# Modulation pieces used a step behind their load in a one-core decoder layer

## The chip, the core and the metric

One core of a Trainium2 chip runs the whole layer as one program. The metric is the device time of one execution in microseconds.

## What is computed

One layer of a hybrid decoder, batch 1, 256 tokens, width 2048, all in float32:

```python
mod = (jax.nn.silu(c) @ w_ada + b_ada)[:, None, :]
sh1, sc1, g1, sh2, sc2, g2 = jnp.split(mod, N_MOD, axis=-1)
h = rms_norm(x, norm1_g) * (1.0 + sc1) + sh1
proj = h @ w_in
...
mixed = jnp.concatenate([rms_norm(attn, attn_out_g), rms_norm(ssm, ssm_out_g)], axis=-1) @ w_out
x = x + g1 * mixed
h2 = rms_norm(x, norm2_g) * (1.0 + sc2) + sh2
ff = jnp.square(jax.nn.relu(h2 @ w_ff1)) @ w_ff2
return x + g2 * ff
```

Between `proj` and `mixed` stand a windowed attention of 8 heads and a state-space branch with a scan. `w_ada` is 2048 x 12288, `w_in` 2048 x 4096, `w_out` 2048 x 2048, `w_ff1` 2048 x 8192 and `w_ff2` 8192 x 2048. The weights come from HBM once, 296 MB in all, 100 MB of them `w_ada`, whose product has a single row.

## The kernel before

**The weights' way.** A load of weights is 512 KB, 128 partitions of 1024 float32. SP issues its DMA into a ring of five buffers with the tag `raw` (`raw`, L176). ACT copies it rounded into `wh` (`copy`, L161), DVE writes the remainder into `wl` (`sub`, called by `split`, L172; the row stands at L136), and PE multiplies with both. So a buffer of the ring is held from the issue of its DMA until DVE has taken `wl` from it. `w_in` is worked off in parts of two loads and 24 matmuls (`w_in_part`, L330), `w_out`, `w_ff1` and `w_ff2` in chunks of one load, 24 matmuls in `pair_bank` (L864) or 16 in `pair_part` (L856). There are 256 feed-forward chunks.

**The modulation.** `w_ada` comes in 96 pieces of 1 MB, four to a block of 512 columns; in this document [b,g] is piece g of block b. They are not loaded in one go but spread over the whole program: `pump` (L285) takes the next pieces of `ADA_ORDER`, and `pump_at(i)` (L578) does so at the rate `PUMPS[i]` for each step of stage i. A piece is loaded into two `raw` buffers, or into one large buffer that is free in that stage (`RINGS`: `PD`, `HA`, `U`, `WB`, or the two halves in `T0`), and used at once: for the blocks in `PE_BLOCKS` by four matmuls of 512 columns (L254), for the others by a scalar_tensor_tensor on DVE with a running sum (L274, whose rows stand at L158).

**The order.** Each engine works its instructions in a fixed order that a scheduler has set when the program was built; an instruction that waits holds up all behind it on its engine. `tc.issue_after(x)` ties an instruction behind x on the same engine.

**The stages.** First the norm of x and the first blocks of `mod` (to 47 us in the profile), then `w_in` against `h`, which `make_h` (L317) makes from x in four groups of 512 channels. From 224 us the scan of the state-space branch runs on DVE beside the last `w_in` parts. Then `y_block` (L693) multiplies the states on PE (L697 and L701), and the attention follows (`att_scores`, L708; `att_values`, L740). `branch_scale` (L831) norms and splits each branch into `CA`, `Q` and `K` for `w_out`. The second norm needs all of `w_out`. Then `ff1_half` (L942) makes the first half of 16 `w_ff1` pairs in eight PSUM banks each, `ff1` the rest, and the four groups of `ff2` follow. `mod` of the last block is needed at the start of the fourth group.

Of the kernel before, what the change touches and what calls it, by code (L numbers as in the profile page):

```python
# [1 line left out]

# [14 lines left out]
P = 128  # L17
SEQ = 256
# [98 lines left out]
class _K:  # L117
    def __init__(self, nc, tc, I, out, pools):
        self.nc, self.tc, self.I, self.out = nc, tc, I, out
        self.sb, self.ps = pools  # L120
        self.n = 0

    def t(self, tag, shape, dt=F32, bufs=1):
        self.n += 1
        return self.sb.tile(list(shape), dt, name=f"{tag}_{self.n}", tag=tag, bufs=bufs)

# [64 lines left out]
    def mm3(self, ps, xh, xl, wh, wl, start, stop):  # L191
        mm = self.nc.tensor.matmul
        mm(ps, xh, wh, start=start, stop=False)  # L193
        mm(ps, xh, wl, start=False, stop=False)  # L194
        mm(ps, xl, wh, start=False, stop=stop)  # L195


def _body(nc, tc, I, out, sb, ps):
# [47 lines left out]
    def ada_pieces(b):  # L246
        c4 = slice(4 * b, 4 * b + 4)
        if b in PE_BLOCKS:
            acc = tr()
            for g in range(4):  # L250
                q = 0
                for raw in ada_raw(I["w_ada"][b, g]):
# [6 lines left out]
                if g < 3:  # L259
                    yield  # L260
            rows = t("rows", [P, NB], bufs=2)
            copy(rows, acc)
            pc = tr()
            for j in range(4):
                mm(pc[:, j : j + 1], rows[:, 128 * j : 128 * j + 128], ones, start=True, stop=True)
            add(mod[:, c4], pc[:, 0:4], col["b_ada"][:, c4])
        else:
            part = t("adap", [P, 2, 4], bufs=2)
            for j in range(4):
                o = 0  # L270
                for i, raw in enumerate(ada_raw(I["w_ada"][b, j])):
                    n = raw.shape[1] * NB
                    rf = raw.rearrange("p a n -> p (a n)")
                    stt(rf, rf, 1.0, cbc[:, o : o + n], ALU.mult, ALU.mult, accum=part[:, i, j : j + 1])  # L274
                    o += n
                if i:
                    add(part[:, 0, j : j + 1], part[:, 0, j : j + 1], part[:, 1, j : j + 1])
                if j < 3:
                    yield
            add(mod[:, c4], part[:, 0], col["b_ada"][:, c4])  # L280
        yield

    state = {"left": 96, "gen": None, "due": 0.0}

    def pump(n=1, until=None):  # L285
        while n > 0 and state["left"] > (96 - until if until is not None else 0):
            if state["left"] % 4 == 0:
                state["gen"] = ada_pieces(ADA_ORDER[24 - state["left"] // 4])
            next(state["gen"])
            state["left"] -= 1  # L290
            n -= 1

    pump(3)

    rw = t("HB", [P, 4, SEQ])
    onek, sel = rw[:, 3, 0:32], rw[:, 3, P : 2 * P]
# [18 lines left out]
    hs = {}  # L315

    def make_h(kg):  # L317
        hs[kg] = t("HA" if kg % 2 == 0 else "HB", [P, 2, 4, SEQ], F32R)
# [522 lines left out]

    xss = branch_scale(("CA",), yg, col["sog"], sq2, 2)
    pump(99, until=48)
    z = t("XT", [P, 16, SEQ])
    for j in range(4):
        nc.sync.dma_start(z[:, 4 * j : 4 * j + 4], I["xT"][:, 4 * j : 4 * j + 4])
# [9 lines left out]
    def pair_part(pp, src, xs, first, last):  # L856
        hi, lo = load_p(src)
        for e in range(2):
            for kk in range(4):
                mm(pp[e], hi[:, e, kk], xs[kk].rearrange("p s n -> p (s n)"), start=first and kk == 0, stop=False)  # L860
            for kk in range(4):
                mm(pp[e][:, 0:SEQ], lo[:, e, kk], xs[kk][:, 0], start=False, stop=last and kk == 3)  # L862

    def pair_bank(bank, src, xs, first, last):  # L864
        hi, lo = load_p(src)
        for e in range(2):
            o = bank[:, SEQ * e : SEQ * e + SEQ]
            for kk in range(4):
                mm(o, hi[:, e, kk], xs[kk][:, 0], start=first and e + kk == 0, stop=False)  # L869
                mm(o, hi[:, e, kk], xs[kk][:, 1], start=False, stop=False)  # L870
            for kk in range(4):
                mm(o, lo[:, e, kk], xs[kk][:, 0], start=False, stop=last and e + kk == 4)  # L872


    def w_out_pair(half, x8, np_):
# [41 lines left out]

    def make_h2(kg):
        pump(99, until=56 + 8 * kg)
        c4 = slice(4 * kg, 4 * kg + 4)  # L920
# [21 lines left out]
    def ff1_half(base):  # L942
# [7 lines left out]
        for i in range(8):  # L950
            copy(part[base + i], banks[i])

    def ff1(np_):
        pp = [k.acc(), k.acc()]
        if np_ % 2 == 0:
            pump(1)
# [3 lines left out]
        aa = ff1_slot(np_)  # L960
# [7 lines left out]
        stt(v, v, 0.0, v, ALU.max, ALU.mult)  # L968
        copy(aa[:, :, 0], v)
        sub(aa[:, :, 1], v, aa[:, :, 0].bitcast(F32))  # L970

    def ff2(G, np_):
        pp = [k.acc(), k.acc()]
# [16 lines left out]

    ff1_half(0)
    ff1_half(8)
    make_h2(2)
    make_h2(3)
    for np_ in range(8):
        ff1(np_)
    y2 = [t("WB2", [P, 8, SEQ]), t("WB3", [P, 8, SEQ])]
    y2 = [y2[c // 8][:, c % 8] for c in range(16)]
    for G in range(4):
# [2 lines left out]
                ff1(8 * G + 8 + np_)  # L1002
        if G == 3:
            pump(99)
            for c in range(16):
                stt(y2[c], y2[c], mod[:, 80 + c : 81 + c], z[:, c], ALU.mult, ALU.add)
        for np_ in range(8):
# [25 lines left out]
```

## Time and profile before

| | us |
|---|---|
| median of three runs | 1293.12 |
| lowest and highest | 1277.10, 1297.98 |
| the profiled execution | 1291.11 |
| its span in the trace | 1289.3 |

The mean granted clock of TensorE over the span is 0.948 of full speed. In the profile's rows a name is that of a tile with its number left out, so `raw<-w_ada` is any load of a piece of `w_ada` into the ring. What stands in square brackets behind a timeline's row is the engine's idle time before it and what released it. In a windows row the order is PE, PEld (weight loads), DVE, ACT, POOL, then the granted clock, the share of the DMA engines and GB/s.

### The profile page before, as it was taken

How to read it: one execution, taken by the hardware profiler on the slowest of the kernel's cores; microseconds unless marked ns; L12 is line 12 of the kernel's file. 1: busy time of each engine (PE TensorE's matmuls, PEld its weight loads, DVE VectorE, ACT ScalarE, POOL GpSimd, SP SyncE). 2: the span in 40 equal slices, each digit the busy share in tenths (PEclk: the TensorE clock that was granted, in tenths of full speed). 3: DMA queues.
4: the chain of work that ended last, by engine and by line, in shares of the span. 5: the costliest groups of instructions: out<-in, count | busy, mean ns of one | idle time of the engine just before them, and what ended most of it. 6: DMA issues, size and time to landing. Idle time of an engine off the chain costs nothing.

```text
span 1289.3 us, 18892 instructions
## 1 busy us (share of the span) xinstructions
PE 1193.7 (93%) x7330; PEld 1012.5 (79%) x7330; DVE 910.5 (71%) x1499; ACT 579.0 (45%) x792; POOL 13.0 (1%) x12
## 2 busy tenths in 40 slices
PE   4688899998998799789989999999999999999998
PEld 1456677863777699789978888888888888888887
DVE  5977697899534985668799655975576666667564
ACT  3588644332145544334354444453344443344432
POOL 1100000000000000000000000000000000000000
PEclk9798999997679899989999999999999999999999
DMA  9785898779155665658997666766677666767663
GB/s 371 286 317 186 280 333 287 274 267 385 36 179 180 239 193 175 210 182 297 327 326 252 203 191 216 262 212 182 195 236 240 225 187 190 219 222 227 202 212 95
DMA packets 77705, 299.64 MB, mean 232 GB/s; under 512 B 8624, under 2 KB 10928, under 8 KB 71856
## 3 DMA queue, kind: packets, MB, share of 16 engines
q1 hardware_dynamic: 77616, 298.45, 69.1%
q8 instruction: 57, 0.93, 0.3%
q14 instruction: 32, 0.26, 0.0%
HBM read 296.31 MB, written 2.10 MB: 231 GB/s over the span
## 4 chain that ended last, share of the span: by engine, by line
PE 60%; DMA 15%; DVE 15%; ACT 5%; issue 4%; SPq 0%; ACTq 0%; DVEq 0%
PE acc L860 31%; PE acc L862 15%; DMA raw<-w_ada 10%; DVE wl L136 4%; DVE raw L158 3%; DVE T L136 2%; PE acc L872 2%; PE acc L870 2%; PE acc L869 2%; PE acc L701 1%; DMA raw<-w_ff 1%; ACT wh L161 1%; PE acc L697 1%; DVE XT L136 1%; ACT TO L161 1%
## 5 line engine op out<-in xcount | busy, mean ns | idle before, releaser
L161 ACT ACTIVATE wh<-raw 128x1024 fp32r<-128x1024 f32 x360 | 381.3, 1060 | 502.1 <-PE acc L860 290.8
L136 DVE TENSOR_TENSOR wl<-raw,wh 128x1024 fp32r<-128x1024 f32 x360 | 439.7, 1223 | 219.0 <-ACT wh L161 217.2
L158 DVE SCALAR_TENSOR_TENSOR raw<-raw,cbc 128x1024 f32<-128x1024 f32 x98 | 119.6, 1225 | 49.3 <-DMA raw<-w_ada 49.0
L860 PE MATMUL acc<-CA,wh 128*128 128x512 f32 x512 | 139.7, 398 | 6.4 <-DVE rows L136 3.4
L860 PEld LDWEIGHTS acc<-CA,wh 128*128 128x128 f32 x512 | 88.4, 190 | 19.2 <-ACT wh L161 4.5
L862 PEld LDWEIGHTS acc<-CA,wl 128*128 128x128 f32 x512 | 76.7, 189 | 10.7
L862 PE MATMUL acc<-CA,wl 128*128 128x256 f32 x512 | 78.2, 278 | 0.0
L860 PE MATMUL acc<-WB,wh 128*128 128x512 f32 x256 | 70.2, 396 | 0.0
L860 PE MATMUL acc<-TO,wh 128*128 128x512 f32 x256 | 70.0, 394 | 0.0
L193 PE MATMUL acc<-wh,HA 128*128 128x512 f32 x128 | 49.8, 417 | 13.2 <-ACT HA L161 9.2
L194 PE MATMUL acc<-wl,HB 128*128 128x512 f32 x128 | 52.6, 411 | 7.1 <-DVE wl L136 7.0
L194 PE MATMUL acc<-wl,HA 128*128 128x512 f32 x128 | 53.2, 416 | 0.9 <-DVE wl L136 0.9
L195 PE MATMUL acc<-wh,HB 128*128 128x512 f32 x128 | 50.6, 400 | 0.0
L195 PE MATMUL acc<-wh,HA 128*128 128x512 f32 x128 | 50.5, 406 | 0.0
L193 PE MATMUL acc<-wh,HB 128*128 128x512 f32 x128 | 47.5, 403 | 1.7 <-ACT wh L161 1.7
L860 PEld LDWEIGHTS acc<-WB,wh 128*128 128x128 f32 x256 | 43.5, 188 | 5.6
L860 PEld LDWEIGHTS acc<-TO,wh 128*128 128x128 f32 x256 | 43.4, 188 | 5.5
L862 PEld LDWEIGHTS acc<-WB,wl 128*128 128x128 f32 x256 | 39.1, 188 | 5.9
L862 PEld LDWEIGHTS acc<-TO,wl 128*128 128x128 f32 x256 | 38.9, 188 | 5.8
L193 PEld LDWEIGHTS acc<-wh,HA 128*128 128x128 f32 x128 | 25.1, 198 | 22.4 <-ACT HA L161 9.3
L862 PE MATMUL acc<-WB,wl 128*128 128x256 f32 x256 | 40.8, 281 | 0.0
L862 PE MATMUL acc<-TO,wl 128*128 128x256 f32 x256 | 39.8, 277 | 0.0
(322 smaller groups left out, 2352.0 us busy)
## 6 DMA issues: line engine op xcount, KB each, us to landing
raw<-w_ff SPq DMA_DIRECT2D x256, 512.0 KB, 4.3
raw<-w_ada SPq DMA_DIRECT2D x98, 512.0 KB, 5.2
raw<-w_in SPq DMA_DIRECT2D x64, 512.0 KB, 6.0
raw<-w_out SPq DMA_DIRECT2D x32, 512.0 KB, 3.8
HA<-w_ada SPq DMA_DIRECT2D x11, 1024.0 KB, 7.3
PD<-w_ada SPq DMA_DIRECT2D x9, 1024.0 KB, 4.9
Q<-w_ada SPq DMA_DIRECT2D x5, 1024.0 KB, 10.3
K<-w_ada SPq DMA_DIRECT2D x5, 1024.0 KB, 8.7
```

What stands on the lines that cost most here:

```text
L136: return (eng or self.nc.vector).tensor_tensor(out, a, b, op=op)
L158: self.nc.vector.scalar_tensor_tensor(out, a, s, b, op0=op0, op1=op1, accum_out=accum)
L161: self.last_act = self.nc.scalar.activation(out, a, AF.Copy, scale=scale).ins
L193: mm(ps, xh, wh, start=start, stop=False)
L194: mm(ps, xh, wl, start=False, stop=False)
L195: mm(ps, xl, wh, start=False, stop=stop)
L697: mm(pv[:, r - r8], toep[:, r].rearrange("p g s j -> p (g s j)"), u2[:, :, r, :], start=True, stop=False)
L860: mm(pp[e], hi[:, e, kk], xs[kk].rearrange("p s n -> p (s n)"), start=first and kk == 0, stop=False)
L862: mm(pp[e][:, 0:SEQ], lo[:, e, kk], xs[kk][:, 0], start=False, stop=last and kk == 3)
L869: mm(o, hi[:, e, kk], xs[kk][:, 0], start=first and e + kk == 0, stop=False)
L870: mm(o, hi[:, e, kk], xs[kk][:, 1], start=False, stop=False)
L872: mm(o, lo[:, e, kk], xs[kk][:, 0], start=False, stop=last and e + kk == 4)
```

## The change

A piece of `w_ada` is now made in two steps. `ada_piece` issues the load and stops; its use follows at the next call of `pump`, or when `drain` is called: ahead of every tile whose tag is in `PLACES`, in `make_h` and `make_h2`, and behind each `pump` with an `until`. The use is tied behind the last main matmul (PE) or the last split's subtraction (DVE) that has been written by then. The tag `T0` is no longer a place for pieces, and the last rate is 0.4 instead of 0.5.

```diff
-RINGS = (('Q', 'K'), ('raw',), ('T0', 'PD', 'raw', 'raw'), ('T0', 'raw', 'raw'), ('raw',), ('HA', 'U', 'WB0'), ('HA', 'PD'))
-PUMPS = (2.0, 2.0, 1.0, 1.0, 1.0, 1.0, 1.0, 0.5, 0.5, 2.5, 1.0, 2.0, 1.0, 0.5)
+PLACES = ("Q", "K", "U", "V", "TO", "CA", "PD", "HA", "WB0")
+RINGS = (('Q', 'K'), ('raw',), ('PD', 'raw', 'raw'), ('raw',), ('raw',), ('HA', 'U', 'WB0'), ('HA', 'PD'))
+PUMPS = (2.0, 2.0, 1.0, 1.0, 1.0, 1.0, 1.0, 0.5, 0.5, 2.5, 1.0, 2.0, 1.0, 0.4)
...
     def split(self, hi, lo, v):
         self.copy(hi, v)
-        return self.sub(lo, v, hi.bitcast(F32))
+        r = self.sub(lo, v, hi.bitcast(F32))
+        self.last_split = r.ins
+        return r
...
+    def ada_piece(b, g):
         c4 = slice(4 * b, 4 * b + 4)
+        raws = ada_raw(I["w_ada"][b, g])
+        yield
         if b in PE_BLOCKS:
...
+            with behind("last_main"):
+                for raw in raws:
...
         else:
...
+            with behind("last_split"):
+                for i, raw in enumerate(raws):
...
     def pump(n=1, until=None):
+        drain()
         while n > 0 and state["left"] > (96 - until if until is not None else 0):
-            if state["left"] % 4 == 0:
-                state["gen"] = ada_pieces(ADA_ORDER[24 - state["left"] // 4])
-            next(state["gen"])
+            drain()
+            i = 96 - state["left"]
+            piece = ada_piece(ADA_ORDER[i // 4], i % 4)
+            next(piece)
+            pending.append(piece)
```

`make_h` takes three steps to a channel group of 128 where it took four:

```diff
             v = xTf[:, kc]
-            mul(v, v, rbc)
-            nc.scalar.activation(v, v, AF.Identity, bias=mod[:, kc : kc + 1], scale=g1c[:, kc : kc + 1])
-            end = k.split(hs[kg][:, 0, kc % 4], hs[kg][:, 1, kc % 4], v)
+            sh = mod[:, kc : kc + 1]
+            stt(v, v, g1c[:, kc : kc + 1], rbc, ALU.mult, ALU.mult)
+            hi = hs[kg][:, 0, kc % 4]
+            k.last_act = nc.scalar.activation(hi, v, AF.Identity, bias=sh).ins
+            end = nc.vector.scalar_tensor_tensor(
+                hs[kg][:, 1, kc % 4], v, sh, hi.bitcast(F32), op0=ALU.add, op1=ALU.subtract
+            )
```

The second half of the first eight `w_ff1` pairs is done in eight PSUM banks, a quarter of the depth for all eight and then the next, with `pump_at(13, 80)` in each step:

```diff
+    def ff1_rest(base):
+        banks = [tr() for _ in range(4)] + [k.acc() for _ in range(4)]
+        for kg in range(2, 4):
+            make_h2(kg)
+            for i in range(8):
+                pair_bank(banks[i], I["w_ff1"][base + i, kg], h2[4 * kg : 4 * kg + 4], kg == 2, kg == 3)
+                pump_at(13, 80)
+        for i in range(8):
+            v = t("rows", [P, 2, SEQ], bufs=2)
+            add(v.rearrange("p e n -> p (e n)"), banks[i], part[base + i])
+            ff1_square(v, base + i)
...
-    make_h2(2)
-    make_h2(3)
-    for np_ in range(8):
-        ff1(np_)
+    ff1_rest(0)
```

**Three places in the order of the engines.** The first is PE at the `y_block`s. Before, in front of them and into the first (`cpad` marks a piece, here [12,0] to [12,2]; the first L701 row is the first block's; `Q`, `K` and the L725 and L726 rows are `att_scores(0)`):

```order
L254 MATMUL tr_2624<-WB_453_2625,cpad_77 32x512 x4
L713 MATMUL tr_2674<-ident_70,Q_818 128x128 x4
L713 MATMUL tr_2680<-ident_70,K_1230 128x128 x4
L254 MATMUL tr_2624<-HA_2764,cpad_77 32x512 x4
L725 MATMUL tr_2687<-WB_430_2423 128x128
L726 MATMUL tr_2687<-WB_430_2423 128x256
L725 MATMUL tr_2699<-WB_430_2423 128x128
L726 MATMUL tr_2699<-WB_430_2423 128x256
L254 MATMUL tr_2624<-U_2830,cpad_77 32x512 x4
L701 MATMUL acc_2439<-XT_1776,CA_378 64x64 x4
L697 MATMUL acc_2439<-PD_1773,TO_374 128x64
L701 MATMUL acc_2439<-XT_1776,CA_378 64x64 x4
```

Now, from the end of the first block to the middle of the second:

```order
L729 MATMUL acc_2414<-PD_1753,TO_370 128x64
L733 MATMUL acc_2414<-XT_1756,CA_374 64x64 x4
L271 MATMUL tr_2456<-HA_2412,cpad_77 32x512 x4
L271 MATMUL tr_2456<-U_2461,cpad_77 32x512 x4
L271 MATMUL tr_2456<-WB_438_2467,cpad_77 32x512 x4
L733 MATMUL acc_2475<-XT_1756,CA_374 64x64 x4
L729 MATMUL acc_2475<-PD_1753,TO_370 128x64
L733 MATMUL acc_2475<-XT_1756,CA_374 64x64 x4
L729 MATMUL acc_2475<-PD_1753,TO_370 128x64
L733 MATMUL acc_2475<-XT_1756,CA_374 64x64 x4
```

Before, the four pieces of block 10 stood among the last `w_in` matmuls and those of block 11, then [12,0] to [12,2], between these and the first L701; now [10,0] to [10,2] stand behind the first block, [10,3] to [11,3] further on among the blocks, and `att_scores(0)` and [12,0] to [12,2] behind the last one.

The second is DVE at the first `branch_scale`, where `PD` and `HA` with `adap` are pieces of block 13 and `rs` is the norm of the branch. Before:

```order
L158 SCALAR_TENSOR_TENSOR PD_3622,adap_3621<-PD_3622,cbc_72 128x2048
L136 TENSOR_TENSOR T_455_2673<-T_455_2673 128x512
L152 TENSOR_SCALAR rs_2427<-tr_3169 128x2
L166 RECIPROCAL rs_2427<-rs_2427 128x2
L136 TENSOR_TENSOR rs_2427<-rs_2427 128x2 x2
L152 TENSOR_SCALAR rs_2427<-rs_2427 128x2
L136 TENSOR_TENSOR rs_2427<-rs_2427 128x2
L829 COPY rbc_3193<-tr_3194 128x256
L156 SCALAR_TENSOR_TENSOR WB_463_2713<-WB_463_2713,small_61,rbc_3193 128x256 x8
L158 SCALAR_TENSOR_TENSOR PD_3754,adap_3621<-PD_3754,cbc_72 128x2048
L136 TENSOR_TENSOR CA_3198<-WB_463_2713,CA_3198 128x256 x4
L158 SCALAR_TENSOR_TENSOR HA_3751,adap_3621<-HA_3751,cbc_72 128x2048
```

Now:

```order
L141 TENSOR_TENSOR T_453_2648<-T_453_2648 128x512
L157 TENSOR_SCALAR rs_2404<-tr_3144 128x2
L171 RECIPROCAL rs_2404<-rs_2404 128x2
L141 TENSOR_TENSOR rs_2404<-rs_2404 128x2 x2
L157 TENSOR_SCALAR rs_2404<-rs_2404 128x2
L141 TENSOR_TENSOR rs_2404<-rs_2404 128x2
L861 COPY rbc_3168<-tr_3169 128x256
L161 SCALAR_TENSOR_TENSOR WB_462_2693<-WB_462_2693,small_61,rbc_3168 128x256 x8
L141 TENSOR_TENSOR CA_3178<-WB_462_2693,CA_3178 128x256 x8
L762 ISA WB_430_2401,den_3287<-tr_3284,HB_2402 128x128
```

The three pieces are gone from between the norm's steps and from among the `CA` splits; they stand further on, among the `w_out` splits.

The third is SP at the end of the `w_ff1` loads, ahead of the first load of `w_ff2`'s fourth group. Before, the order goes from the last `w_ff1` load to `w_ff2` straight on:

```order
L178 DMA raw_1615_10408<-w_ff1 128x1024
L178 DMA raw_1618_10430<-w_ff1 128x1024
L178 DMA raw_1624_10478<-w_ff2 128x1024
L178 DMA raw_1627_10500<-w_ff2 128x1024
L178 DMA raw_1630_10522<-w_ff2 128x1024
```

Now:

```order
L185 DMA raw_1600_10476<-w_ff1 128x1024
L185 DMA raw_1604_10506<-w_ada 128x1024
L185 DMA raw_1605_10508<-w_ada 128x1024
L185 DMA raw_1607_10514<-w_ada 128x1024
L185 DMA raw_1608_10516<-w_ada 128x1024
L185 DMA raw_1609_10521<-w_ada 128x1024
L185 DMA raw_1610_10523<-w_ada 128x1024
L185 DMA raw_1611_10528<-w_ada 128x1024
L185 DMA raw_1612_10530<-w_ada 128x1024
L185 DMA raw_1615_10554<-w_ff2 128x1024
L185 DMA raw_1618_10576<-w_ff2 128x1024
```

The whole of block 23, eight loads of 512 KB, has come to stand between the two, and its eight DVE instructions likewise.

## Rows read from the trace of the kernel before

**Rows 1.** The page, part 1: engine, busy us (share of the span), instructions.

```profile
PE 1193.7 (93%) x7330; PEld 1012.5 (79%) x7330; DVE 910.5 (71%) x1499; ACT 579.0 (45%) x792; POOL 13.0 (1%) x12
```

**Rows 2.** Windows by stage: length, busy of each engine (instructions), clock, DMA, GB/s.

```profile
126.00:224.00 98.00, 91.04 (x393) 71.93 (x392) 77.49 (x115) 51.48 (x78) 0.22 (x1) 0.97 0.84 296
224.00:330.00 106.00, 95.61 (x497) 65.90 (x495) 99.79 (x160) 35.93 (x43) 0.00 (x0) 0.90 0.81 297
330.00:365.00 35.00, 35.00 (x311) 27.90 (x310) 10.01 (x28) 4.25 (x12) 0.00 (x0) 0.53 0.02 3
...
411.00:464.00 53.00, 45.63 (x319) 41.17 (x320) 44.88 (x96) 28.80 (x57) 0.00 (x0) 0.87 0.68 243
...
538.00:552.40 14.40, 2.83 (x17) 2.27 (x15) 9.89 (x24) 2.44 (x5) 0.00 (x0) 0.70 0.66 219
552.40:704.70 152.30, 141.52 (x1025) 133.22 (x1026) 127.14 (x214) 67.05 (x84) 0.00 (x0) 0.96 0.82 281
704.70:1289.30 584.60, 579.67 (x3330) 505.44 (x3328) 382.52 (x514) 248.75 (x280) 0.00 (x0) 1.00 0.66 206
```

**Rows 3.** The page, part 4: shares of the chain by line.

```profile
PE acc L860 31%; PE acc L862 15%; DMA raw<-w_ada 10%; DVE wl L136 4%; DVE raw L158 3%; DVE T L136 2%; PE acc L872 2%; PE acc L870 2%; PE acc L869 2%; PE acc L701 1%; DMA raw<-w_ff 1%; ACT wh L161 1%; PE acc L697 1%; DVE XT L136 1%; ACT TO L161 1%
```

**Rows 4.** The page, part 5: two DVE lines and ACT's; busy, mean ns, idle before.

```profile
L161 ACT ACTIVATE wh<-raw 128x1024 fp32r<-128x1024 f32 x360 | 381.3, 1060 | 502.1 <-PE acc L860 290.8
L136 DVE TENSOR_TENSOR wl<-raw,wh 128x1024 fp32r<-128x1024 f32 x360 | 439.7, 1223 | 219.0 <-ACT wh L161 217.2
L158 DVE SCALAR_TENSOR_TENSOR raw<-raw,cbc 128x1024 f32<-128x1024 f32 x98 | 119.6, 1225 | 49.3 <-DMA raw<-w_ada 49.0
```

**Rows 5.** The page, part 6: DMA issues; KB each, us to landing.

```profile
raw<-w_ff SPq DMA_DIRECT2D x256, 512.0 KB, 4.3
raw<-w_ada SPq DMA_DIRECT2D x98, 512.0 KB, 5.2
raw<-w_in SPq DMA_DIRECT2D x64, 512.0 KB, 6.0
```

**Rows 6.** Timeline of DVE at the start: start us, us, what.

```profile
37.27 4.44 DVE L136 TENSOR_TENSOR XT<-XT,rbc 128x256 f32<-128x256 f32 x13
...
43.77 0.15 DVE L136 TENSOR_TENSOR mod<-tr,small 128x4 f32<-128x4 f32 x1
```

**Rows 7.** Timeline of PE at the start.

```profile
46.40 0.80 PE L193 MATMUL acc<-wh,HA 128*128 128x512 f32 x1 [9.24 <-ACT HA L161]
```

**Rows 8.** Timeline of PE, 306 to 330 us.

```profile
306.59 1.93 PE L254 MATMUL tr<-WB,cpad 128*32 128x512 f32 x8 [0.29 <-DMA WB<-w_ada]
...
326.69 1.06 PE L254 MATMUL tr<-U,cpad 128*32 128x512 f32 x8
...
329.22 0.45 PE L701 MATMUL acc<-XT,CA 64*64 64x64 f32 x8 [1.47 <-DVE XT L136]
```

**Rows 9.** Windows of 6 us around the scan's end.

```profile
308.00:314.00 6.00, 2.46 (x12) 0.20 (x8) 5.86 (x14) 0.00 (x0) 0.00 (x0) 0.50 1.02 425
...
326.00:332.00 6.00, 4.53 (x53) 2.85 (x51) 5.86 (x17) 1.38 (x7) 0.00 (x0) 1.00 0.49 175
...
332.00:338.00 6.00, 6.00 (x56) 4.94 (x58) 5.93 (x16) 1.08 (x3) 0.00 (x0) 0.51 0.01 3
```

**Rows 10.** Timeline of DVE behind the attention, 419 to 435 us.

```profile
419.90 2.29 DVE L158 SCALAR_TENSOR_TENSOR PD<-PD,cbc 128x2048 f32<-128x2048 f32 x1 [2.95 <-DMA PD<-w_ada]
...
429.11 2.29 DVE L158 SCALAR_TENSOR_TENSOR PD<-PD,cbc 128x2048 f32<-128x2048 f32 x1
...
432.66 2.28 DVE L158 SCALAR_TENSOR_TENSOR HA<-HA,cbc 128x2048 f32<-128x2048 f32 x1
```

**Rows 11.** Timeline of DVE at the second norm, 537 to 550 us.

```profile
537.59 1.23 DVE L158 SCALAR_TENSOR_TENSOR raw<-raw,cbc 128x1024 f32<-128x1024 f32 x1 [2.58 <-DMA raw<-w_ada]
...
546.57 1.23 DVE L158 SCALAR_TENSOR_TENSOR raw<-raw,cbc 128x1024 f32<-128x1024 f32 x1 [2.04 <-DMA raw<-w_ada]
...
547.99 1.22 DVE L158 SCALAR_TENSOR_TENSOR raw<-raw,cbc 128x1024 f32<-128x1024 f32 x1
```

More of the change, by code (lines that the diff above doesn't have):

```diff
@@ L1 @@
+import contextlib
 import math
@@ L120, in __init__ @@
         self.sb, self.ps = pools
+        self.drain = None
         self.n = 0
     def t(self, tag, shape, dt=F32, bufs=1):
+        if self.drain and tag in PLACES:
+            self.drain()
         self.n += 1
@@ L194, in mm3 @@
         mm(ps, xh, wl, start=False, stop=False)
-        mm(ps, xl, wh, start=False, stop=stop)
+        self.last_main = mm(ps, xl, wh, start=False, stop=stop).ins
 def _body(nc, tc, I, out, sb, ps):
@@ L244, in ada_raw, with behind @@
         return [k.raw(src[:, 2 * NB * i : 2 * NB * i + 2 * NB].rearrange("p (a n) -> p a n", a=2), tag) for i in range(2)]
-    def ada_pieces(b):
+    def behind(name):
+        ins = getattr(k, name, None)
+        return tc.issue_after(ins) if ins is not None else contextlib.nullcontext()
+    accs_ada = {}
+    def ada_piece(b, g):
         c4 = slice(4 * b, 4 * b + 4)
+        raws = ada_raw(I["w_ada"][b, g])
+        yield
         if b in PE_BLOCKS:
[L249 to L252, printed above, removed]
+            if g == 0:
+                accs_ada[b] = tr()
+            acc = accs_ada[b]
+            q = 0
+            with behind("last_main"):
+                for raw in raws:
                     for i in range(raw.shape[1]):
@@ L258, in ada_pieces @@
                         q += 1
[L259 to L266, printed above, removed]
-        else:
[L268 to L271, printed above, removed]
+            if g == 3:
+                rows = t("rows", [P, NB], bufs=2)
+                copy(rows, acc)
+                pc = tr()
+                for j in range(4):
+                    mm(pc[:, j : j + 1], rows[:, 128 * j : 128 * j + 128], ones, start=True, stop=True)
+                add(mod[:, c4], pc[:, 0:4], col["b_ada"][:, c4])
+        else:
+            if g == 0:
+                accs_ada[b] = t("adap", [P, 2, 4], bufs=2)
+            part = accs_ada[b]
+            o = 0
+            with behind("last_split"):
+                for i, raw in enumerate(raws):
@@ L272, in ada_pieces @@
                     n = raw.shape[1] * NB
                     rf = raw.rearrange("p a n -> p (a n)")
-                    stt(rf, rf, 1.0, cbc[:, o : o + n], ALU.mult, ALU.mult, accum=part[:, i, j : j + 1])
+                    stt(rf, rf, 1.0, cbc[:, o : o + n], ALU.mult, ALU.mult, accum=part[:, i, g : g + 1])
                     o += n
                 if i:
-                    add(part[:, 0, j : j + 1], part[:, 0, j : j + 1], part[:, 1, j : j + 1])
-                if j < 3:
-                    yield
@@ L280, in ada_pieces, with drain @@
-            add(mod[:, c4], part[:, 0], col["b_ada"][:, c4])
+                    add(part[:, 0, g : g + 1], part[:, 0, g : g + 1], part[:, 1, g : g + 1])
+                if g == 3:
+                    add(mod[:, c4], part[:, 0], col["b_ada"][:, c4])
         yield
-    state = {"left": 96, "gen": None, "due": 0.0}
+    state = {"left": 96, "due": 0.0}
+    pending = []
+    def drain():
+        while pending:
+            next(pending.pop(0))
     def pump(n=1, until=None):
+        drain()
@@ L317, in make_h @@
     def make_h(kg):
+        drain()
         hs[kg] = t("HA" if kg % 2 == 0 else "HB", [P, 2, 4, SEQ], F32R)
@@ L700, in y_block @@
                     pr = slice(64 * gp, 64 * gp + 64)
-                    mm(
+                    k.last_main = mm(
                         pv[pr, r - r8], ca[pr, r, ri].rearrange("p s j -> p (s j)"), H[pr, ri, r, :],
                         start=False, stop=ri == 1,
-                    )
+                    ).ins
         copy(yv[:, :, r8 : r8 + 8], pt.rearrange("p (r h c) -> p h r c", r=8, h=2))
@@ L843, in _body @@
     pump(99, until=48)
+    drain()
     z = t("XT", [P, 16, SEQ])
@@ L861, in pair_part @@
             for kk in range(4):
-                mm(pp[e][:, 0:SEQ], lo[:, e, kk], xs[kk][:, 0], start=False, stop=last and kk == 3)
+                k.last_main = mm(pp[e][:, 0:SEQ], lo[:, e, kk], xs[kk][:, 0], start=False, stop=last and kk == 3).ins
     def pair_bank(bank, src, xs, first, last):
@@ L871, in pair_bank @@
             for kk in range(4):
-                mm(o, lo[:, e, kk], xs[kk][:, 0], start=False, stop=last and e + kk == 4)
+                k.last_main = mm(o, lo[:, e, kk], xs[kk][:, 0], start=False, stop=last and e + kk == 4).ins
     def w_out_pair(half, x8, np_):
@@ L919, in make_h2 @@
         pump(99, until=56 + 8 * kg)
+        drain()
         c4 = slice(4 * kg, 4 * kg + 4)
@@ L932, in _body @@
     pump(99, until=64)
+    drain()
     ring["tags"] = ("raw",)
@@ L951, in ff1_half, with ff1_square @@
             copy(part[base + i], banks[i])
+    def ff1_rest(base):
[9 more added lines that the diff above has]
+            ff1_square(v, base + i)
+    def ff1_square(v, np_):
+        aa = ff1_slot(np_)
+        stt(v, v, 0.0, v, ALU.max, ALU.mult)
+        copy(aa[:, :, 0], v)
+        sub(aa[:, :, 1], v, aa[:, :, 0].bitcast(F32))
     def ff1(np_):
         pp = [k.acc(), k.acc()]
-        if np_ % 2 == 0:
-            pump(1)
+        pump(1 if np_ % 2 == 0 else 0)
         kgs = range(2, 4) if np_ < 16 else range(4)
@@ L1004, in _body @@
             pump(99)
+            drain()
             for c in range(16):
```

7 lines of the change are left out of this document (3 added, 4 removed).

## The prediction

> **What bounds the kernel now.** I read the page's shares first: PE is busy 93% of the span [rows 1], so only the other 7%, and stretches in which PE is slow, can give anything back. The windows by stage come next, because the mean hides where the 7% lie. From 704.7 us to the end PE is busy 579.67 of 584.60 us at full clock [rows 2]: whatever is won ahead of that point stays won, and almost nothing can be won behind it. In the stages before, the same view shows PE short of work: 7.0 us idle of 98.0 in the `w_in` stage (126 to 224 us), 10.4 of 106.0 beside the scan, 7.4 of 53.0 around the first `branch_scale`, 11.6 of 14.4 at the second norm, 10.8 of 152.3 in the first feed-forward chunks. Third, the chain: 10% of the span, some 129 us of 1289.3, is a load of `w_ada` on its way into the ring, and another 3% the DVE instruction that uses it [rows 3]. That is work nobody is in need of yet, yet it stands at the head of DVE's queue: its 98 instructions found DVE idle 49.0 us for their loads [rows 4]. Behind each of them waits a `wl`, and behind that PE. The `w_in` part is 24 matmuls, so 393 PE instructions are 16 parts of 6.1 us; a feed-forward chunk at the end costs 584.60 / 208 = 2.81 us (256 less the 48 done by 704.7), and each of the 48 before that 152.3 / 48 = 3.17 us.
>
> The sum below is made against the profiled execution, 1291.1 us (1.8 more than its span). The median of the three runs is 2.0 us above that. From no change the measurement of this kernel tells about 2%, 26 us.
>
> **The change, part by part.** *Start.* Before, DVE did 13 multiplications of `XT` in 4.44 us and three more ahead of the `mod` addition, and PE stood 9.24 us until the first `HA` was there at 46.40 [rows 6, 7]. In the new order only two `wl` (1.22 us each [rows 4]) and four scalar_tensor_tensor on `XT` stand between the norm's last step and that addition, from 36.05 (37.27 less the `wl` ahead of it) some 36.05 + 2.4 + 4 x 0.5 = 40.5 us instead of 43.77 (0.5 is an estimate above 4.44 / 13 = 0.34, for the two-step operation), and behind it one ACT step instead of two. I take 4.5 us (bounds 0 and 5). ACT does 16 steps less in all, which I cost at nothing: it was idle 502 us ahead of `wh` alone [rows 4].
>
> *The ring in the `w_in` stage.* A buffer of the ring is held while its load lands (6.0 us for `w_in`, 5.2 for `w_ada` [rows 5]), and until ACT (1.06) and DVE (1.22) are through: 8.3 us for weights, 6.4 for a piece, 7.35 in the mean. With four loads to a part, five buffers give one part in 4 x 7.35 / 5 = 5.9 us, and 6.1 was measured: the ring sets the pace, DVE's wait is one form in which it shows. The change takes the piece out of the head of DVE's queue, but keeps it until the next part's split, and puts two more pieces into the ring, because `T0` is gone. Holding gets longer, the wait on DVE shorter; I take 0 (bounds -7, all PE idle there, and +16, which is the rival below). The scan behind it keeps its work on DVE, busy 99.79 of 106.0 us [rows 2]; 0, and -6 if the idle rest goes.
>
> *The pieces among the `y_block`s.* This is the loss. Before, pieces of blocks 10 to 12 ran on PE while it waited for the scan: one took 1.93 us at half clock and 1.06 at full, and the first L701 was released by the scan at 329.22 [rows 8]. They cost nothing. Now eleven of them stand behind the scan, eight among the `y_block`s, where PE is busy 35.00 of 35.00 us [rows 2]. Eight are 8.5 us at full clock and 15.5 at half; I take the middle, 12, and 1 more for the last three, which mostly lie in the wait of PE for the transposes behind. +13 (bounds +21, eleven at half clock, and -6, the rival on the clock).
>
> *First `branch_scale`.* The piece that kept DVE idle 2.95 us and then busy 2.29 stood ahead of the branch's norm, and two more of 2.29 and 2.28 among the `CA` splits that `w_out` waits for [rows 10]. In the new order the norm and the eight splits follow each other. The sum is 9.8 us, and the pieces go into the `w_out` stage, where DVE has room. -9.5 (bounds -5, as only the first surely lies on the path, and -10).
>
> *Second norm.* Two pieces' halves, 2.04 us of wait, 1.23 and 1.22 us, stood between the steps of the norm, and another with a wait of 2.58 us ahead of the last split of `w_out` [rows 11]. The first three sum to 4.5 on the path, the other counts in part. -5.5 (bounds -4 and -8).
>
> *First 48 feed-forward chunks.* The ring again: at one piece to two chunks, two chunks bring four loads, in 6.35 us, so a buffer is held 5 x 6.35 / 4 = 7.9 us. At the new rate five chunks bring nine loads: 9 x 7.9 / 5 = 14.2 us, 2.85 a chunk instead of 3.17, just above PE's own 2.81. That would be 48 x 0.32 = 15 us. As the two groups of `make_h2` still stand among them and DVE was busy 127 of 152 us, I take two thirds, -10 (bounds -17, PE's pace, and +8, the rival). In the same rows the transfers ran at 281 GB/s. The Trainium skill, DMA: Bandwidth & Descriptors, section Specifications, gives about 358 GB/s as what HBM yields one core; four loads in 5.62 us would ask 373, so by that rule the transfers bound the stage, 5.86 us for two chunks, and the lower rate would bring only 24 x 0.24 = 5.8 us, in all 1282. The trace disagrees: 425 GB/s in a window of 6 us [rows 9].
>
> *The last block.* The lower rates leave block 23 for the end: eight loads go between the last `w_ff1` and the first load of the fourth `ff2` group. When DVE starts the last `w_ff1` split, PE has three chunks left, 8.4 us. The eight pass a ring of five: four are there, four come 4.3 to 5.2 us after a buffer is free, at one per 1.22 us; the load behind them is issued after some 6.1 us, lands at 10.4 and is `wh` at 11.5. PE waits 3 us, and a little for `wl`: +4 (bounds 0 and 6). `pair_bank` instead of `pair_part` in 16 chunks has the same columns, 0.
>
> **Sum.** -4.5 + 0 + 13 - 9.5 - 5.5 - 10 + 4 = -12.5, so 1291.1 - 12.5 = 1278.6; I say **1278 us**.
>
> **Rivals.** *The pieces wake the clock.* In the window of 326 to 332 us the granted clock was at the full 2.4 GHz, behind pieces and transposes in close order; six us on, in `y_block`s alone, it was at 0.51, almost all at 1.2 GHz, though PE was busy 6.00 of 6.00 us [rows 9]. With `y_block`s alone the clock fell; with pieces between them it might not. At full clock the `y_block`s would take 17.5 us and eleven pieces 11.7, 29 instead of 35: -6 in place of +13, 1259 us. The Trainium skill, TensorE: Matmul & The Clock Gate, section on the HAM clock gate, says that throttled is the default state and that activity releases it; by that rule this rival is the one to expect, and the trace bears out the release at 326 but not that a busy PE keeps it. Against it: five of the eight stand singly, 1.9 us each, between long runs of small matmuls. Chance 0.13.
>
> *The ring is relieved wholly.* The waits of DVE were the cause and not a form of the ring's: PE's idle 7 us in the `w_in` stage and 6 of DVE's beside the scan go, and the chunks run at PE's pace, 7 more: 1258 us. For it speaks that the waits on pieces make 49 us [rows 4]; against it, that buffers are then held longer. Chance 0.17.
>
> *The ring starves: slower than before.* A piece now stays in its two buffers until the next step's split has passed. If it is held 3 us longer than before (half a `w_in` part, about one chunk), the mean hold in the `w_in` stage is 8.85 us, a part takes 4 x 8.85 / 5 = 7.1 us, 16 parts 16 us more; in the chunks 4 of 9 buffers make it 9.2 us, 16.6 for five chunks, 3.3 each, +8 instead of -10. That is 34 us worse, 1312. It decides from about 1.1 us longer: there it has eaten the 12.5. Against it: landing takes 5.2 us, longer than a chunk, so most of the step's delay is spent on landing anyway. Chance 0.16.
>
> **How the numbers follow.** The forecast has 0.54, its own range 1266 to 1291 from the middle halves of its bounds. The range over all cases, 1252 to 1303, reaches both fast rivals and half way into the slow one. Faster by over 2% (under 1267) come nearly all of the fast rivals and a tenth of the forecast: 0.31. Slower by over 2% (over 1319) is only the slow rival with a longer hold: 0.06. Within 2% remains 0.63.
>
> **What would show it.** Right: DVE's waits on `w_ada` loads fall from 49 us to below 15; PE's first `w_in` matmul comes at 41 to 42 us; from the first L733 to the last, 45 to 50 us instead of 35; 5 to 6 us less at the second norm; 2.9 to 3.0 us per chunk in the first 48; a gap of 3 to 5 us ahead of the fourth `ff2` group. Wrong: a full clock among the `y_block`s, or parts of 7 us in the `w_in` stage with ACT waiting for `w_in` loads.

## The result and the profile after

The changed kernel takes 1356.6 us in the median of four runs (1354.7 to 1362.5), the kernel before beside it 1295.0: a ratio of 1.056, interval 1.044 to 1.069. The forecast was 1278 us and the range ended at 1303. The profiled execution took 1354.7 us with a span of 1352.9, 63.6 us more than the span before. (Ratios leave out runs more than 1.5% above the fastest of their kernel, which matters below where a kernel's times fall in two groups.)

First the page of the changed kernel, parts 1 and 5, against [rows 1, 4]:

```profile
PE 1199.2 (89%) x7458; PEld 1025.2 (76%) x7458; DVE 908.7 (67%) x1472; ACT 573.4 (42%) x776; POOL 13.0 (1%) x12
...
L141 DVE TENSOR_TENSOR wl<-raw,wh 128x1024 fp32r<-128x1024 f32 x360 | 438.8, 1222 | 324.8 <-ACT wh L166 323.4
L166 ACT ACTIVATE wh<-raw 128x1024 fp32r<-128x1024 f32 x360 | 381.1, 1060 | 585.2 <-PE acc L893 277.9
L163 DVE SCALAR_TENSOR_TENSOR raw<-raw,cbc 128x1024 f32<-128x1024 f32 x102 | 120.8, 1219 | 1.8 <-DMA raw<-w_ada 1.8
```

PE's busy time has hardly changed, 1199.2 us against 1193.7; its share fell from 93% to 89% because it waits more. DVE's wait for the pieces is gone, from 49 us to 1.8 in 102 instructions. In its place `wl` waits longer for `wh`, 324.8 us instead of 219.0, and `wh` itself, on ACT, 585.2 instead of 502.1. What ACT waits for stands in the view of waits (us in total, times, longest). Before:

```profile
DVE wl L136 <- ACT wh L161: 217.2, 181, 4.0
...
DVE raw L158 <- DMA raw<-w_ada: 49.0, 43, 3.0
...
ACT wh L161 <- DMA raw<-w_in: 31.1, 17, 5.1
...
ACT wh L161 <- DMA raw<-w_ff: 29.1, 15, 5.1
```

After:

```profile
DVE wl L141 <- ACT wh L166: 323.4, 214, 8.7
...
ACT wh L166 <- DMA raw<-w_ff: 96.7, 35, 7.0
ACT wh L166 <- DMA raw<-w_in: 78.7, 37, 8.2
```

The waiting has moved to loads of weights: ACT waits 78.7 us for `w_in` and 96.7 for `w_ff` where it waited 31.1 and 29.1, 115 us more in all, against 64 us that the kernel lost; the rest of this waiting went by while PE had work. Loads did not land more slowly (6.1 and 4.3 us, against 6.0 and 4.3 in [rows 5]); they were issued later.

The windows by stage, against [rows 2]:

```profile
117.00:235.00 118.00, 96.78 (x385) 73.98 (x384) 80.26 (x117) 49.65 (x72) 0.21 (x1) 0.90 0.73 251
235.00:355.00 120.00, 80.28 (x393) 64.79 (x391) 108.23 (x173) 35.20 (x41) 0.00 (x0) 0.84 0.60 205
355.00:393.00 38.00, 37.55 (x394) 25.37 (x395) 8.47 (x15) 3.10 (x6) 0.00 (x0) 0.84 0.57 208
...
439.00:490.00 51.00, 45.52 (x337) 41.11 (x336) 30.44 (x82) 32.59 (x64) 0.00 (x0) 0.90 0.41 136
...
566.60:574.00 7.40, 2.70 (x13) 2.30 (x12) 4.41 (x13) 2.03 (x5) 0.00 (x0) 0.65 0.38 129
574.00:755.00 181.00, 153.05 (x1153) 147.22 (x1154) 115.00 (x179) 67.06 (x85) 0.00 (x0) 0.91 0.67 227
755.00:1352.90 597.90, 584.01 (x3328) 508.27 (x3326) 395.63 (x539) 247.93 (x281) 0.00 (x0) 0.99 0.67 210
```

The `w_in` stage has become 118.0 us instead of 98.0, and it holds less work: its 385 PE instructions are 335 matmuls of `w_in` and 48 transposes, those before were 359 and 32. For the same fifteen parts, the ninth to the twenty-third, PE takes 125.3 us (from 125.4) instead of 98.3 (from 128.4). Of these 27.0 us PE is idle for 16.2 and busy longer for 10.8, at a mean granted clock of 0.88 instead of 0.97. The 48 chunks take 181.0 us instead of 152.3, with 17.2 us more of idle PE and 11.5 more of busy PE, at 0.91 instead of 0.96. So idle time is the larger part of the loss, and a lower clock goes with it. In the scan's stage PE is idle 39.7 us instead of 10.4. Following a few matmuls and the scan's first step through both timelines gives the lateness at each point:

| point | before, us | after, us | later by | this stretch |
|---|---|---|---|---|
| first `w_in` matmul | 46.4 | 39.6 | -6.8 | -6.8 |
| first scan step on DVE | 235.4 | 257.4 | +22.0 | +28.8 |
| first matmul of the `y_block`s behind the scan | 329.2 | 355.5 | +26.2 | +4.2 |
| end of the last `y_block` matmul | 364.0 | 392.9 | +28.9 | +2.7 |
| first `w_glu` matmul | 372.5 | 407.3 | +34.8 | +5.9 |
| end of the last `w_out` matmul | 538.6 | 566.6 | +28.1 | -6.7 |
| first `w_ff1` matmul | 552.4 | 574.1 | +21.7 | -6.4 |
| 48 chunks done | 704.7 | 755.0 | +50.3 | +28.6 |
| first matmul of the fourth `ff2` group | 1196.1 | 1257.9 | +61.8 | +11.5 |
| end | 1289.3 | 1352.9 | +63.6 | +1.8 |

Two stretches make up 57 of the 64 us, and both are those in which the ring carries the most pieces beside the weights.

How a piece starves the weights can be read in one part of the `w_in` stage, from all engines' timelines (start us, us, engine, what; SPq is the issue of a DMA):

```profile
121.70 4.59 SPq L185 DMA_DIRECT2D raw<-w_ada  x2
...
127.07 1.23 DVE L141 TENSOR_TENSOR wl<-raw,wh 128x1024 fp32r<-128x1024 f32 x1 [1.13 <-ACT wh L166]
...
128.21 1.22 DVE L163 SCALAR_TENSOR_TENSOR raw<-raw,cbc 128x1024 f32<-128x1024 f32 x1
128.32 1.47 SPq L185 DMA_DIRECT2D raw<-w_in  x2
...
132.54 1.06 ACT L166 ACTIVATE wh<-raw 128x1024 fp32r<-128x1024 f32 x1 [0.20 <-DMA raw<-w_in]
...
133.63 1.23 DVE L141 TENSOR_TENSOR wl<-raw,wh 128x1024 fp32r<-128x1024 f32 x1 [0.75 <-ACT wh L166]
...
135.37 1.06 ACT L166 ACTIVATE wh<-raw 128x1024 fp32r<-128x1024 f32 x1 [1.29 <-DMA raw<-w_in]
...
136.46 1.23 DVE L141 TENSOR_TENSOR wl<-raw,wh 128x1024 fp32r<-128x1024 f32 x1 [1.60 <-ACT wh L166]
...
137.61 1.22 DVE L163 SCALAR_TENSOR_TENSOR raw<-raw,cbc 128x1024 f32<-128x1024 f32 x1
```

The first half of a piece is issued at 121.70. With it the ring is full, and the second half follows at 125.97, into the next buffer that comes free. SP can issue the first of the next part's two loads only at 128.32, when the second `wl` of the part before (127.07) is through, and the other when a half of the piece before that (DVE, 128.21) has been used. ACT waits 0.20 and 1.29 us for them and takes them at 132.54 and 135.37, the second split starts at 136.46, and only behind it, at 137.61, comes the piece's first instruction, because it is tied to that split. It had held its buffer for 15.9 us by then. From 125.97 until 129.43 this piece and the one before it held four of the five buffers, and the loads that the release hangs on had one. Pairing every issue in this stage (117 to 230 us) with the DVE instruction that empties the buffer, half a piece holds its buffer for 15.6 us in the mean (20 buffers); before (126 to 224 us) it was 8.4 (17 buffers of the ring). In the 48 chunks it is 12.2 us instead of 7.2.

### The profile page after: what moved, and what is told of

The parts are those of the page before. It is cut to its first block, busy times and chain, and to the rows that moved or that the text cites. A ratio compares the mean times of both kernels' runs of the same rounds, so it can differ in the third digit from the quotient of the medians.

```text
span 1352.9 us, 19049 instructions
## 1 busy us (share of the span) xinstructions
PE 1199.2 (89%) x7458; PEld 1025.2 (76%) x7458; DVE 908.7 (67%) x1472; ACT 573.4 (42%) x776; POOL 13.0 (1%) x12
## 4 chain that ended last, share of the span: by engine, by line
PE 61%; DMA 13%; DVE 13%; ACT 8%; issue 4%; SPq 0%; ACTq 0%; DVEq 0%
PE acc L893 27%; PE acc L895 13%; DMA raw<-w_ff 7%; DMA raw<-w_in 5%; DVE raw L163 4%; DVE wl L141 3%; ACT wh L166 3%; PE acc L903 3%; PE acc L902 3%; PE acc L905 3%; DVE T L141 1%; PE tr L271 1%; DMA V<-w_ada 1%; PE acc L733 1%; PE tr L582 1%
## 5 line engine op out<-in xcount | busy, mean ns | idle before, releaser
L141 DVE TENSOR_TENSOR wl<-raw,wh 128x1024 fp32r<-128x1024 f32 x360 | 438.8, 1222 | 324.8 <-ACT wh L166 323.4
L166 ACT ACTIVATE wh<-raw 128x1024 fp32r<-128x1024 f32 x360 | 381.1, 1060 | 585.2 <-PE acc L893 277.9
L893 PE MATMUL acc<-CA,wh 128*128 128x512 f32 x384 | 105.9, 398 | 4.5 <-DVE rows L141 4.5
L893 PEld LDWEIGHTS acc<-CA,wh 128*128 128x128 f32 x384 | 65.7, 189 | 13.7 <-issue 4.5
L200 PE MATMUL acc<-wh,HA 128*128 128x512 f32 x128 | 51.3, 435 | 17.8 <-ACT wh L166 12.4
L895 PEld LDWEIGHTS acc<-CA,wl 128*128 128x128 f32 x384 | 59.1, 190 | 8.7
L895 PE MATMUL acc<-CA,wl 128*128 128x256 f32 x384 | 60.3, 280 | 0.0
L202 PE MATMUL acc<-wh,HA 128*128 128x512 f32 x128 | 52.5, 417 | 0.0
L902 PE MATMUL acc<-CA,wh 128*128 128x256 f32 x192 | 47.2, 281 | 0.7 <-ACT wh L166 0.7
L200 PEld LDWEIGHTS acc<-wh,HA 128*128 128x128 f32 x128 | 25.8, 208 | 28.8 <-ACT wh L166 19.4
L903 PE MATMUL acc<-CA,wh 128*128 128x256 f32 x192 | 47.0, 281 | 0.3 <-DVE CA L141 0.3
```

The source lines that it names most:

```text
L141: return (eng or self.nc.vector).tensor_tensor(out, a, b, op=op)
L166: self.last_act = self.nc.scalar.activation(out, a, AF.Copy, scale=scale).ins
L202: self.last_main = mm(ps, xl, wh, start=False, stop=stop).ins
L895: k.last_main = mm(pp[e][:, 0:SEQ], lo[:, e, kk], xs[kk][:, 0], start=False, stop=last and kk == 3).ins
```

## The experiments

Theory 1 was the third rival of the prediction, with the traces behind it: the pieces, held a step longer in five buffers, starve the weights. Against it stood the other parts of the change: the missing place `T0`, the lower rate with `ff1_rest`, and the tie as such.

**Pieces at once again (now_all).**

```diff
     def behind(name):
-        ins = getattr(k, name, None)
-        return tc.issue_after(ins) if ins is not None else contextlib.nullcontext()
+        return contextlib.nullcontext()
...
-            pending.append(piece)
+            next(piece)
```

> The changed kernel, but every piece is used at once behind its load and tied to nothing, as before; the new places, rates, make_h and ff1_rest stay. Theory 1 (a piece that lies a step longer in the ring of five starves the weights' loads): the w_in stage and the first 48 feed-forward chunks get back the some 32 and 30 us that they lost, the gains at the first branch_scale and the second norm (13) go, the pieces leave the y_blocks (-11): 1290 to 1305 us; mean hold of a piece in the ring of 126 to 224 us back from 17 to about 9 us. Rival (the loss comes from the missing place T0, the rate and ff1_rest): 1330 us or more, holds at 9 us all the same.

Measured: 1283.6 and 1307.7 us, mean 1295.6, and a mean hold of a piece in the ring of the `w_in` stage of 8.6 us. The places, the rate and `ff1_rest` were those of the changed kernel, so the late use with its tie costs 49 to 73 us; untied, below, gives 58 from eight runs. Its waits are those of the kernel before again, DVE's on pieces at 75.0 us even above it:

```profile
DVE raw L163 <- DMA raw<-w_ada: 75.0, 44, 4.6
...
ACT wh L166 <- DMA raw<-w_ff: 43.0, 19, 5.4
...
ACT wh L166 <- DMA raw<-w_in: 35.3, 19, 5.8
```

The head-of-line wait on DVE, which I wanted gone, and the short hold are the same thing seen from two sides: DVE stands ready when the piece lands, and the buffer is free 1.2 us later. (tie_now, below, shows that they can be had apart in part.)

**At once only in the ring (now_ring), and there only in the first half (now_win).**

```diff
+        ring["last"] = tag
...
             pending.append(piece)
+            if ring["last"] == "raw":
+                drain()
```

(and no tie in that case; now_win adds `and state["left"] > 48`).

> The changed kernel, but a piece that lies in the ring is used at once and untied; pieces in the large buffers stay a step behind. Theory 1: both starved stages recover, the gain at the first branch_scale and at the start stays, that at the norm goes in part: 1280 to 1298 us. Rival (places, rate, ff1_rest): 1320 us or more.

> As now_ring for the first 48 pieces alone (up to the first branch_scale); behind that the pieces in the ring stay a step behind their load. Theory 1: only the w_in stage recovers, some 32 us: 1318 to 1330 us, with the first 48 feed-forward chunks still at some 181 us. If the w_in loss came from the missing T0, it stays near 1355.

now_ring: 1304.4 us, ratio to before 1.009 (1.006 to 1.012), 6 us above what was expected; both starved stages recovered, and much of the rest is what the feed-forward part costs (before_ff, below). now_win: 1329.7 us, as theory 1 said, with the 48 chunks as slow as in the changed kernel, 181.7 us:

```profile
547.30:729.00 181.70, 152.94 (x1157) 146.22 (x1158) 115.73 (x179) 68.04 (x84) 0.00 (x0) 0.92 0.68 226
```

So each of the two stages starves by itself, and each recovers by itself. `T0` has no part in it: now_all, without it, begins the scan at 226.2 us, and before_h (below), with it and the same `make_h`, at 226.2 and 224.9.

**The tie.** untied takes away only the ties, with the use still written a step behind the load; tie_now keeps the ties but writes the use at once, so that the tie is to the split of the same step.

> The changed kernel, a step behind the load, but tied to no split or matmul, so that the scheduler may put the use earlier. If the tie holds the buffers, the mean hold of a piece falls towards 9 us and the time below 1310; if the order in which the step is written does (theory 1 without the tie), the hold stays above 14 us and the time within 10 us of 1356.

> The changed kernel with the ties kept, but each piece used at once behind its load, so that it is tied to the split (or matmul) of the step in which it was loaded and not to the next step's. If what starves the ring is the next step's split, which itself waits for two loads that need the ring, the mean hold of a piece in the ring (w_in stage) is below 11 us and the time 1288 to 1308 us, near now_all and untied; if any tie behind a split does it, the hold stays above 14 us and the time above 1330.

untied: 1298.4 us (1.004, 0.999 to 1.009), hold 7.9 us: without the tie the scheduler puts the use where the load lands, whatever the order in which it was written. tie_now: 1302.3 us (1.008, 1.002 to 1.014), hold 10.4 us. DVE's wait for pieces is 5.3 us in it, ACT's for `w_in` 59.1:

```profile
ACT wh L166 <- DMA raw<-w_in: 59.1, 26, 5.7
...
DVE raw L163 <- DMA raw<-w_ada: 5.3, 7, 1.3
```

It is the tie to the next step's split that does the harm, not a tie as such. In the `w_in` stage the wait taken from DVE comes back on ACT: the same fifteen parts take 105.6 us, against 93.4 in now_all. In the 48 chunks it does not: they take 147.7 us, against 160.0 in now_all and 152.3 before, with a hold of 8.0 us against 7.1 in now_all. That is one trace, but it is the gain that the change was made for, from a tie that makes the hold only 0.9 us longer. It is lost again behind the 48 chunks, where this trace loses 14.7 us against that of before, 8.9 of them at the fourth `ff2` group.

**A sixth buffer (raw6_wl2).**

```diff
-RAW = 5
+RAW = 6
...
-        lo = self.t("wl", [P, 2, NB], F32R, bufs=3)
+        lo = self.t("wl", [P, 2, NB], F32R, bufs=2)
```

(the same in `load_p`).

> The changed kernel with six buffers in the ring instead of five; to make room wl has two instead of three, which can only cost. If the ring is what the late pieces starve, the sixth buffer gives back a good part of the 60 us: 1310 to 1340 us. If it is the order of DVE's instructions, the time stays at 1356 or rises.

Measured: 1315.1 us (two runs), 41 us less than the changed kernel, although `wl` lost a buffer. DVE's order is that of the changed kernel, a piece is held 17.7 us in the `w_in` stage, longer than ever, and the waits for weights fall:

```profile
ACT wh L166 <- DMA raw<-w_ff: 85.4, 43, 6.6
ACT wh L166 <- DMA raw<-w_in: 60.3, 27, 6.1
```

Both stages gain: the scan begins at 240.6 us instead of 257.4, and the 48 chunks take 156.8 us instead of 181. That is the ring itself: with the hold left as it is, the buffers decide.

**make_h alone (before_h, twice).** The kernel before with the three-step `make_h` as in the diff above.

> The kernel before with the three-step make_h alone. The start's term (4.5 us forecast, 7.7 read from the two traces) says 1284 to 1290 us; if what is won at the start is lost again to the ring in the w_in stage, 1294.

> The same kernel as before_h, for its second profile and its spread. If the two groups of times seen in it and in the kernel before (some 13 us apart) come from TensorE's clock in the y_blocks, a profiled run at 1280 us or more has that stretch (first to last L702 matmul) at half clock and some 35 us long, one at 1276 or less at full clock and some 23 us; a run in the upper group with a 23 us stretch contradicts it.

1281.7 us (0.992, 0.987 to 0.997), 2 us less than was expected, and 1271.9 in a second set on another chip (0.987, 0.980 to 0.994). It takes less time than either kernel. The start brings 8 to 10 us in its traces (last matmul of the fourth `w_in` part at 68.3 and 66.2 instead of 76.1), and it is not lost again in the `w_in` stage. Both of its profiles, 1269.3 and 1271.0 us, fell in the lower group of times and show the `y_block`s at full clock (line 705 in that kernel); none in the upper group was profiled, so the expectation was tested on one side only. ACT waits 98.9 us for loads of `w_in` and `w_ff` in the first trace, 39 more than before, in a faster kernel: this wait by itself is no measure of a loss.

**The feed-forward part alone (before_ff).** The kernel before with the rate 0.4 and `ff1_rest`.

> The kernel before with the rate 0.4 and ff1_rest alone, pieces used at once. The forecast's step (a lower rate relieves the ring, -10, tail +4) says 1284 to 1290 us; now_all's trace (6 us lost in the first 32 chunks, 4 ahead of ff2, 5 at the tail) says 1300 to 1310.

Median 1305.5 us of ten runs. The ratio, 0.996 (0.988 to 1.004), rests on the two lowest alone and decides nothing. The times fall in two groups, like those of the kernel before beside it: 1283.4 and 1289.6 us against 1279.0 to 1280.0, and 1303.2 to 1312.0 (median 1305.6) against 1292.7 to 1302.1 (median 1295.7). Group against group it is 7 to 10 us slower. Its trace, with the `y_block`s at half clock as in that of before, shows where: it is 4.2 us early in the first `w_ff1` chunks, 2.4 late behind the 48, 5.8 late ahead of the fourth `ff2` group and 12.1 behind that group's first chunks, so the part costs some 16 us in this trace, 6 of them at the last block, where PE waits:

```profile
1205.63 3.78 PE L860 MATMUL acc<-V,wh 128*128 128x512 f32 x8 [3.54 <-ACT wh L161]
```

**What is worth keeping (mix, twice).** The changed kernel with the step behind the load for pieces 52 to 67 alone, all others at once and untied, and the feed-forward part of before.

> The changed kernel with the step behind the load kept only for pieces 52 to 67 (blocks 16, 13, 17, 14: those used from the first branch_scale to the second norm, where few loads contend for the ring); all others are used at once and untied, and the feed-forward part is that of before (rate 0.5, no ff1_rest). If the gains that the two traces show at the start (8), the first branch_scale (7) and the second norm (6) are kept without the starved stages: 1268 to 1282 us. If the gain at the branch needed the pieces among the y_blocks, 1282 to 1290.

> The same kernel as mix, timed in more rounds on one chip with before_h: 1270 to 1282 us, 1 to 1.5% below the kernel before; below before_h_b by 3 to 8 us if the gains at the first branch_scale and the second norm stay, equal if they are lost again in the first feed-forward chunks.

1277.9 us (0.988, 0.979 to 0.998) and 1279.8 (0.988, 0.982 to 0.994): it takes less time than either kernel. Against before_h, which has the make_h edit alone, it is 3.8 us lower beside it on the first chip and 7.9 higher on the second, so the late pieces are not shown to bring anything. In its first trace it is level with before_h's at the last `w_out` chunk, 5.0 us ahead at the first `w_ff1` chunk, behind the second norm, and 0.4 ahead 32 chunks on. Whether the late use is worth anything over the whole kernel stays open.

## Why the prediction was wrong

**What held.** DVE's wait fell from 49 us to 1.8, as forecast. The start, forecast -4.5 (bounds 0 and 5), brought -6.8:

```profile
39.56 0.80 PE L200 MATMUL acc<-wh,HA 128*128 128x512 f32 x1 [3.58 <-ACT HA L354]
```

The first `branch_scale`, -9.5, brought -6.7; the second norm, -5.5, brought -6.4. The last block was forecast at +4 with a bound of 6; the cause came as forecast, somewhat larger: PE waits 5.5 us for `wh` and loses 1.8 more in the chunk behind:

```profile
1257.93 3.78 PE L893 MATMUL acc<-V,wh 128*128 128x512 f32 x8 [5.52 <-ACT wh L166]
```

**The step that failed** is the ring in the `w_in` stage, "I take 0", with the sentence that was to hold it up: landing takes longer than a chunk, "so most of the step's delay is spent on landing anyway". It compared the landing of the piece with the length of a chunk. But the use is not released by time; it is released by the next step's second split, which waits for two loads that themselves wait for buffers, then land, and pass ACT and DVE. One landing is covered, the second is not: 15.6 us of hold, not 6.4 plus 3. The rival had the mechanism right. Its own hold (3 us longer) was less than half of what came (7.1 us longer, 5.0 in the chunks), so its 1312 us and the range's 1303 both fell short. The term was -7 to +16 and measured +27.0 over the same fifteen parts, +28.8 up to the scan. Both signs that were to show the forecast wrong came: parts of 8.4 us with ACT waiting for `w_in`, and a full clock among the `y_block`s.

That the prediction's model gave the pace of the kernel before, 5.9 us a part, was luck. The 393 PE instructions of the window are 15 parts and 32 transposes, so a part took 6.5 us and not 6.1. The ring carried 46 loads for them, three to a part and not four, as pieces also went to `PD` and `T0`; and a buffer was held 10.6 us in the mean (8.4 for pieces, 11.9 for weights) and not 7.35. Too many loads and too short a hold nearly made up for each other. Nor does such a sum show what bounds a stage. SP fills a buffer again as soon as it is free, so the mean number of buffers held is 4.98 to 4.99 of five in the `w_in` stage and the 48 chunks of both kernels, and still 4.93 before and 4.96 after in the last stage, where PE is busy over 97% of the time.

**The 48 chunks**, -10, measured +28.6, by the same step and by one more: the lower rate brings nothing where pieces are used at once and untied. before_ff and now_all lose some 7 us there; tie_now alone gained. The lower rate also took fewer loads of pieces out of the stretch than the forecast had it: 36 before, 31 in the changed kernel. 7.1 us of the changed kernel's loss is a single gap, PE waiting for the last quarter of `h2`; the last half piece of its modulation was issued at 717.14 us, and two splits stood on DVE between its use and the sum:

```profile
729.78 1.01 PE L902 MATMUL tr<-CA,wh 128*128 128x256 f32 x3 [7.09 <-ACT CA L962]
```

**The pieces among the `y_block`s**, +13, cost 2.7 us among the blocks and 5.9 behind them, with `att_scores(0)`. The rival on the clock was half right. Six-us windows of the changed kernel:

```profile
356.00:362.00 6.00, 6.00 (x52) 4.87 (x50) 5.79 (x10) 0.00 (x0) 0.00 (x0) 0.50 0.00 0
...
368.00:374.00 6.00, 6.00 (x80) 4.32 (x73) 0.00 (x0) 0.00 (x0) 0.00 (x0) 1.00 0.90 362
...
386.00:392.00 6.00, 6.00 (x67) 4.28 (x68) 0.00 (x0) 0.60 (x1) 0.00 (x0) 1.00 0.91 325
```

The first block ran at half clock (0.50); behind the three pieces after it the clock was full and stayed so to the last block. Eight pieces in 2.7 us net means that the full clock paid for most of them. Pieces among the blocks did not always keep it: in tie_now, with as many among them, it rose at 343.0 us, fell to half at 349.9 and rose again at 353.3. The scan, taken as 0, cost 4.2; PE stood for it longer than for anything else in either trace:

```profile
355.45 0.69 PE L733 MATMUL acc<-XT,CA 64*64 64x64 f32 x8 [26.45 <-DVE XT L141]
```

But 22.0 of the 26.2 us of lateness at this point had been made before the scan began; the gap is so wide because the pieces that once filled it now stand behind.

The rule of the Trainium skill weighed ahead (DMA: Bandwidth & Descriptors, Specifications, some 358 GB/s) would have given 1282 us; the changed kernel's 48 chunks moved 227 GB/s, less than that rule's figure and than the 281 of before, so transfers did not bound them.

## What to carry to other kernels

A buffer in a shared ring is taken from its issue to its release. Taking a wait off an engine by using the data later lengthens that time, and where the ring has nothing to spare the wait comes back at the loads behind. Before such a delay is written, ask what releases the use: if it is an event that needs buffers of the same ring, the hold is two landings and not one. The shortest tie that takes the use out of the engine's way is the one to try first, as the 48 chunks of tie_now suggest.

A long hold is no loss by itself, and a full ring is no proof that the ring is the bound. Behind the 48 chunks and ahead of the last block the changed kernel holds pieces for 19.5 us, where the kernel before held them for 5.5, and from 770 to 1250 us PE is busy 476.5 of 480.0 us. What tells is whether PE stands waiting in that stage for what the ring brings, and what one buffer more gives back.

## What the runs showed of the hardware

The kernel before has two groups of times. Of the 17 runs beside mix_b two took 1278.3 and 1282.2 us with a mean granted clock of 0.963 and 0.964, and fifteen 1291.8 to 1300.2 with 0.946 to 0.954. The traces show one place that can make such a step. In the profiled run of before, TensorE's clock falls to 0.51 at 332 us, among the `y_block`s, with PE busy all the time [rows 9], and these last 34.8 us. In before_h, whose order of these matmuls is the same, the clock was full when they began and stayed so:

```profile
320.00:326.00 6.00, 5.99 (x82) 4.74 (x86) 6.00 (x22) 2.26 (x9) 0.00 (x0) 1.00 0.13 53
326.00:332.00 6.00, 6.00 (x84) 4.46 (x78) 4.43 (x7) 0.31 (x1) 0.00 (x0) 1.00 0.51 175
332.00:338.00 6.00, 6.00 (x95) 4.99 (x92) 0.00 (x0) 0.87 (x2) 0.00 (x0) 1.00 0.01 3
```

They took 23.1 us from 320.0 to 343.1. The same held in now_all, untied, before_h_b and mix (22.0 to 23.1 us), so 12 us hang on whether the clock falls there. mix_b, the very program of mix, was profiled in a run of 1293.5 us and shows the other case, 36.1 us, at 0.50 from 327.7 us on; so does before_ff, 36.5 us. The Trainium skill, TensorE: Matmul & The Clock Gate, section on the HAM clock gate, has throttled as the default state that activity releases. The trace agrees that the clock rose behind dense work (0.50 ahead of the three pieces of the changed kernel, 1.00 behind them), and shows beside it that the same small matmuls, back to back, kept it in some executions and lost it in others. What decides it is not shown. Just ahead of the first of them PE stood idle 1.5 us in before [rows 8], 1.6 in mix_b and 2.6 in before_ff, which lost the clock, and 0.8 to 1.3 us in the five traces that kept it; but no run changed this idle time alone.

With the pieces among the blocks the times of the changed kernel and of now_ring lie close together (1354.7 to 1362.5, and 1301.4 to 1306.4), but those of tie_now, with as many pieces among them, do not (1293.1 to 1315.2); that this order makes the time steadier is not shown.
